# Streamed modulation summed on TensorE in four column blocks, and second buffers for the operands of a recurrent head

## The chip, the cores and the metric

The kernel runs on one core of one Trainium2 chip. The metric is the device time of one execution in microseconds (us); lower is better. "Before" was timed in three runs. Engines are named as the profile names them: PE is TensorE, DVE is VectorE, ACT is ScalarE, POOL is GpSimd, SP is SyncE, whose instruction queue issues nearly all DMAs of this kernel.

## What is computed

One step of a two-layer diffusion trunk over 512 sample tokens and 128 prompt tokens, 2048 features, all in float32. Each layer first turns a conditioning vector into a shift, a scale and a gate for every feature, once for the sample and once for the prompt:

```python
def modulate_and_norm(x, cond, w_mod, b_mod, g):
    m = (jax.nn.silu(cond) @ w_mod + b_mod)[:, None, :]
    shift, scale, gate = jnp.split(m, 3, axis=-1)
    return rmsnorm(x, g) * (1 + scale) + shift, gate
```

`w_mod` is [2048, 6144] in each layer, 50 MB, and it multiplies two vectors only. The first layer then has eight heads of latent attention and eight heads of a gated recurrence run in both directions (chunked scan: queries, values, two forget gates, a state per head), the second has sixteen heads of attention in a window; each ends in an output projection, a gate and a residual sum.

## The kernel before

Activations lie with features on the partitions and the 640 tokens along the row. Wide products run as `coltile`: 128 output columns at a time, in two *units* of eight 128-row weight tiles (512 KB). A unit's weights come by one DMA into a buffer of the pool `rawp` (four buffers, L149), are split into a high and a low part by one ACT copy (L75) and one DVE subtraction (L76), and are used by 48 matmuls of 320 columns in three passes (L113 to L115). The results gather in PSUM banks named `acc`.

The stages follow one another: the start (modulation of layer one for the features needed at once, `mod_tensor`, L267, and the first columns); the eight recurrent heads (`hgrn_head`); the latent attention; the output of layer one; layer two.

The change lies in the stage of the recurrent heads. A head needs five `coltile` products, ten units: two gates (evicted by ACT, L490, into the tile `e`), the query (evicted by DVE, L477, into `q`), the value (`v`, after a transpose) and the output gate. Between them stands its recurrence: some 60 elementwise operations of DVE and ACT, and small matmuls (L554, L556, L580, L611, L625 to L628) that each wait for DVE. Four levels of a doubling scheme follow one another: the small products of a level (L580), a masked copy (L552), then a multiplication of queries (L589) and keys (L590) by decays. `e` is overwritten by the keys and lives until the last transposes of the head; `e`, `q` and `v` have one buffer each, so the next head's gates can't be evicted before.

Beside the heads runs the *stream*: the modulation sums that are not needed at once, 4 blocks of 512 features of layer one and all 12 of layer two. `mod_sums` (L280) keeps them off PE. Each of its 128 pieces loads 512 KB into `mraw` (two buffers); for each of the two row tiles in it DVE multiplies by the sample's conditioning and adds (L295), ACT multiplies by the prompt's (L296) and POOL adds (L297). After eight pieces four matmuls against ones sum over the partitions (L302), one for each quarter of the accumulators, into four 32-column blocks of PE side by side; an ACT copy (L305) and two DMAs (L307) put the 512 sums in DRAM. `pump` (L320), called once a unit, advances the stream by eight pieces in five units.

The order of work within each engine is fixed when the program is built, by a scheduler that goes by program order and its own estimates of time; every engine, and the SP queue, then runs its list in order, waiting on semaphores. Weight splits are placed ahead of their place in the program (`ahead`). PSUM has eight banks; in this stage three are `acc`, three are for short-lived results (`w`) and two for the heads' outputs (`o`).

Of the kernel before, what the change touches and what calls it, by code (L numbers as in the profile page):

```python
# [14 lines left out]
P = 128  # L15
D = 2048
KT = 16
# [11 lines left out]
class Trunk:  # L29
# [20 lines left out]
    def rsqrt(self, out, v, tmp, add):  # L50
        """out = (v + add) ** -0.5; v may be in PSUM, tmp is scratch of the same shape."""
# [15 lines left out]
    def sigmoid(self, out, x):  # L67
        """out = 1 / (1 + exp(-x)), x bounded below."""
        nc = self.nc
        nc.scalar.activation(out, x, AF.Exp, scale=-1.0)  # L70
        nc.scalar.activation(out, out, AF.Ln, bias=self.bias_of(1.0, out.shape[0]))
        nc.scalar.activation(out, out, AF.Exp, scale=-1.0)
# [5 lines left out]
    def token_sums(self, pool, parts):  # L78
        """Sums over the features for (columns of ones [128, 32], squares [128, 640]) parts -> [128, 5], by token."""
# [15 lines left out]
    def unit(self, src, pool=None, **kw):  # L95
        """src: AP [128, k, n] in DRAM -> split tile [128, 2, k, n]."""
# [9 lines left out]
    def ahead(self):  # L106
        """What is emitted inside is scheduled before its place in the program."""
        return self.tc.high_priority(offset=400)

    def three(self, out, w, a, start, stop):  # L110
        """out (+)= w.T @ a with w, a = (hi, lo) pairs."""
# [5 lines left out]
    def coltile(self, w, c0, act, us=(0, 1), extra=0):  # L117
        """(w[:, c0:c0+128]).T @ act -> two PSUM tiles, the first with the extra leading columns of act."""
# [18 lines left out]
    def banked(self, **banks):  # L137
        """PSUM banks of a phase by use: w short-lived, o sums of heads, m modulation, acc wide products."""
# [6 lines left out]
    def setup(self):  # L145
# [22 lines left out]
        for l in ("ab", "c"):  # L168
            self.mod[l] = self.t(c, [P, 48, 2], tag=f"mod_{l}")
            # gains (1 + scale) * norm  # L170
            self.mod[l + "a"] = self.t(c, [P, 16, 2], tag=f"moda_{l}")

    def conditioning(self, tp):
        """silu of the two conditionings, as stationary columns 0 and 1."""
# [28 lines left out]
    def gains(self, tp):  # L203
# [24 lines left out]
        # lower bounds of the forget gates: softmax over the layer axis, cumulated, minus its first row  # L228
# [16 lines left out]
    def mod_done(self, l, f0, n, ps):  # L245
        """Feature tiles f0 .. f0+n from their sums in ps [128, n, 2]."""
# [10 lines left out]
    def mod_tensor(self, l, js):  # L257
        """Features 256*j .. on the tensor engine, four blocks of rows side by side; yields after each piece."""
# [21 lines left out]
    def mod_sums(self, l, js, pool):  # L280
        """Features 512*j .. summed over blocks of rows off the tensor engine; yields after each piece."""
        nc = self.nc
        wm = self.io[f"mod_w_{l}"][0].rearrange("(k p) c -> p k c", p=P)
        for j in js:
            acc = self.t(pool, [P, 2, 512], tag="macc")
            for kq in range(8):
                raw = self.t(pool, [P, 2, 512], tag="mraw", bufs=2)
                nc.sync.dma_start(raw, wm[:, 2 * kq:2 * kq + 2, 512 * j:512 * j + 512])
                for i in range(2):
                    s0, s1 = (self.sc[:, 2 * kq + i, c:c + 1] for c in range(2))  # L290
                    if kq + i == 0:
                        nc.vector.tensor_scalar(acc[:, 0], raw[:, i], scalar1=s0, scalar2=None, op0=ALU.mult)
                        nc.scalar.activation(acc[:, 1], raw[:, i], AF.Copy, scale=s1)
                    else:
                        nc.vector.scalar_tensor_tensor(acc[:, 0], raw[:, i], s0, acc[:, 0], op0=ALU.mult, op1=ALU.add)  # L295
                        nc.scalar.activation(raw[:, i], raw[:, i], AF.Copy, scale=s1)  # L296
                        nc.gpsimd.tensor_tensor(acc[:, 1], acc[:, 1], raw[:, i], op=ALU.add)  # L297
                if kq < 7:
                    yield
            ps = self.w()[:, :256]  # L300
            for g in range(4):
                nc.tensor.matmul(ps[32 * g:32 * g + 32, :], lhsT=self.ones[1.0][:, 0:32],  # L302
                                 rhs=acc[:, g // 2, 256 * (g % 2):256 * (g % 2) + 256], start=True, stop=True)
            row = self.t(pool, [P, 256], tag="mrow")
            nc.scalar.activation(row, ps, AF.Copy)  # L305
            for c in range(2):
                nc.sync.dma_start(self.mrow[c, 2 * j:2 * j + 2], row[64 * c:64 * c + 64:32])  # L307
            if j == 11:
                f0 = 4 * js[0]
                n = 48 - f0  # L310
                rows = self.t(pool, [2 * n, P], tag="mrows")
                for c in range(2):
                    nc.sync.dma_start(rows[n * c:n * c + n], self.mrow[c, 2 * js[0]:24].rearrange("a (i p) -> (a i) p", p=P))
# [6 lines left out]
    def pump(self):  # L320
        """One product unit passes: the share of the streamed modulation that goes with it."""
        if self.stream is not None:
            self.units += 1
            for _ in range(2 if self.units % 5 in (0, 2, 4) else 1):
                next(self.stream, None)

# [36 lines left out]
    def start(self):  # L363
# [6 lines left out]
        def columns(k0, k1, c):  # L370
            """Rows 128*k0 .. 128*k1 of w_in, one tile of the latent and gate columns."""
# [32 lines left out]
        def modulate(k):  # L404
            """h tile k (hi, lo)."""
# [26 lines left out]
    def latent_norm(self, xs, j0, gain):  # L432
        """Latent rows j0 .. normalised over the features, to DRAM."""
# [25 lines left out]
    def hgrn_setup(self, pool):  # L459
        nc, io = self.nc, self.io  # L460
        self.masks = self.t(pool, [P, 6, P], U8, tag="masks")
        stage = self.t(pool, [P, 6, P], tag="e")
# [8 lines left out]
    def evict_silu(self, pool, pts, tag):  # L471
        """(bounded x) * sigmoid(x) of a column tile."""
        nc = self.nc
        x = self.t(pool, [P, T], tag=tag)
# [849 lines left out]
```

## Time and profile before

| | us |
|---|---|
| runs timed | 2556.28, 2563.78, 2561.87 |
| median | 2561.87 |
| profiled execution, first to last instruction (its span; no other time of it is recorded) | 2554.8 |
| of it, the stage of the recurrent heads with the stream: first piece loaded to last sums read back | 849 (231 to 1080) |

The table's last row is a stretch of the profiled execution. Busy times, idle times and durations below all come from that one execution. A group row reads: line, engine, operation, tiles written and read, count, then busy time, mean duration, idle time just before and what ended it. A PE instruction's end is modelled and overlaps the next one's start, so the cost of a matmul in a row of them is read from the distance between starts. A float32 matmul appears as two records, one in the high-and-low product (L113 to L115) as one.

### The profile page before, as it was taken

The page shows a single profiled execution, that of the slowest core. Times are in us where ns is not written, and L with a number is a line of the kernel's source. Part 1 is how long each engine was busy: PE and PEld are TensorE (multiplying, and loading weights), DVE is VectorE, ACT ScalarE, POOL GpSimd, SP SyncE. Part 2 cuts the span into 40 slices and gives each one's busy share as a digit, 9 for nine tenths or more (in the row PEclk, how much of TensorE's full clock was granted, in tenths as well). Part 3 has the DMA queues.
Part 4 walks back from the last instruction along what each step waited for, and adds up shares of the span by engine and source line. Part 5 has one row for each costly group of instructions (what it writes and reads, how often), then busy time and mean ns, then how long its engine had stood idle before and what let it go on. Part 6 is the DMA issues. An engine that isn't in the chain of part 4 may idle for free.

```text
span 2554.8 us, 42083 instructions
## 1 busy us (share of the span) xinstructions
PE 2443.2 (96%) x16745; PEld 2319.2 (91%) x16745; DVE 1644.2 (64%) x3002; ACT 1088.2 (43%) x1979; POOL 465.2 (18%) x313
## 2 busy tenths in 40 slices
PE   7999898998989888999999999999999999999999
PEld 5789888888888888898898999999999999999999
DVE  4656889889888898857555566555555555564222
ACT  4224544554545445445444343344344343354211
POOL 1001545554545555300000012000000000000000
PEclk8999999999999999999999999999999999999999
DMA  9974444444444444454233355322222222225431
GB/s 309 303 246 153 139 124 144 136 143 128 137 133 148 138 128 136 121 147 141 72 99 100 110 189 157 108 72 72 84 77 74 82 73 70 80 55 165 120 116 58
DMA packets 409124, 324.94 MB, mean 127 GB/s; under 512 B 36218, under 2 KB 347936, under 8 KB 408416
## 3 DMA queue, kind: packets, MB, share of 16 engines
q1 hardware_dynamic: 408352, 322.17, 41.8%
q8 instruction: 131, 2.15, 0.3%
q14 instruction: 65, 0.53, 0.1%
q0 software_dynamic: 576, 0.09, 0.1%
HBM read 277.58 MB, written 36.76 MB: 123 GB/s over the span
## 4 chain that ended last, share of the span: by engine, by line
PE 57%; DVE 4%; DMA 1%; issue 1%; ACT 0%; POOL 0%; SPq 0%; DVEq 0%; POOLq 0%; ACTq 0%
PE acc L114 14%; PE acc L115 14%; PE acc L113 14%; PE w L48 2%; PE w L113 2%; PE o L1150 2%; PE w L115 2%; PE w L114 2%; PE o L897 1%; DVE macc L295 1%; PE w L874 1%; DVE split L76 1%; DMA mraw<-in_mod_w_c_dram 1%; PE w L84 0%; PE w L873 0%
## 5 line engine op out<-in xcount | busy, mean ns | idle before, releaser
L113 PE MATMUL acc<-act,split 128*128 128x320 f32 (+1 forms) x3552 | 1131.1, 319 | 29.1 <-DVE q L477 27.2
L115 PE MATMUL acc<-act,split 128*128 128x320 f32 (+1 forms) x3552 | 1122.9, 316 | 0.0
L114 PE MATMUL acc<-act,split 128*128 128x320 f32 (+1 forms) x3552 | 1122.6, 316 | 0.1
L113 PEld LDWEIGHTS acc<-act,split 128*128 128x128 f32 x3552 | 680.9, 192 | 63.6 <-DVE q L477 29.3
L114 PEld LDWEIGHTS acc<-act,split 128*128 128x128 f32 x3552 | 680.2, 192 | 6.9 <-issue 2.7
L115 PEld LDWEIGHTS acc<-act,split 128*128 128x128 f32 x3552 | 680.4, 192 | 5.8 <-issue 3.3
L297 POOL TENSOR_TENSOR macc<-macc,mraw 128x512 f32<-128x512 f32 x240 | 411.7, 1716 | 390.4 <-ACT mraw L296 250.4
L75 ACT ACTIVATE split<-raw 128x1024 fp32r<-128x1024 f32 (+4 forms) x297 | 284.3, 957 | 433.5 <-PE acc L115 412.9
L76 DVE TENSOR_TENSOR split<-raw,split 128x1024 fp32r<-128x1024 f32 (+4 forms) x297 | 348.7, 1174 | 182.1 <-ACT split L75 174.9
L295 DVE SCALAR_TENSOR_TENSOR macc<-mraw,sc,macc 128x512 f32<-128x512 f32 x240 | 246.7, 1028 | 65.9 <-DMA mraw<-in_mod_w_c_dram 44.0
L296 ACT ACTIVATE mraw<-mraw,sc 128x512 f32<-128x512 f32 x240 | 172.7, 722 | 240.5 <-DVE macc L295 194.7
L580 PE MATMUL w<-lf,km 128*128 128x128 f32 x320 | 46.7, 298 | 40.9 <-DVE lf L589 40.6
L1133 ACT ACTIVATE sc<-sc,mxc,rqc 128x512 f32<-128x512 f32 (+2 forms) x80 | 56.1, 701 | 67.2 <-DVE mxc L1132 67.1
L580 PEld LDWEIGHTS w<-lf,km 128*128 128x128 f32 x320 | 41.7, 205 | 46.6 <-ACT mraw L296 23.7
L114 PE MATMUL acc<-mc,split 128*128 128x320 f32 x256 | 80.2, 314 | 0.2 <-DVE mc L76 0.2
L113 PE MATMUL acc<-mc,split 128*128 128x320 f32 x256 | 79.1, 314 | 0.0
L115 PE MATMUL acc<-mc,split 128*128 128x320 f32 x256 | 79.0, 309 | 0.0
L113 PE MATMUL acc<-mixa,split 128*128 128x320 f32 x256 | 78.8, 308 | 0.0
L114 PE MATMUL acc<-mixa,split 128*128 128x320 f32 x256 | 78.8, 308 | 0.0
L115 PE MATMUL acc<-mixa,split 128*128 128x320 f32 x256 | 78.7, 308 | 0.0
L388 DVE TENSOR_TENSOR lat<-lat,acc 128x320 f32<-128x320 f32 (+1 forms) x72 | 34.9, 485 | 58.4 <-PE acc L115 58.1
L648 DVE TENSOR_TENSOR swc<-swc,tabC 128x512 f32<-128x512 f32 x20 | 13.9, 693 | 85.3 <-DMA swc<-qc 69.1
(395 smaller groups left out, 3478.6 us busy)
## 6 DMA issues: line engine op xcount, KB each, us to landing
mraw<-in_mod_w_c_dram SPq DMA_DIRECT2D x96, 512.0 KB
raw<-in_w_in_ab_dram SPq DMA_DIRECT2D x92, 512.0 KB
raw<-in_w_in_c_dram SPq DMA_DIRECT2D x80, 512.0 KB
raw<-in_mod_w_ab_dram SPq DMA_DIRECT2D x64, 512.0 KB
mraw<-in_mod_w_ab_dram SPq DMA_DIRECT2D x32, 512.0 KB
raw<-in_w_out_ab_dram SPq DMA_DIRECT2D x32, 512.0 KB
raw<-in_w_out_c_dram SPq DMA_DIRECT2D x32, 512.0 KB
raw<-in_w_in_ab_dram SPq DMA_DIRECT2D x24, 256.0 KB
```

Source lines behind the costliest of these rows:

```text
L48: self.nc.tensor.transpose(out, in_, self.ident[:k, :k])
L75: self.nc.scalar.activation(hi, full, AF.Copy)
L76: self.nc.vector.tensor_tensor(lo, full, hi.bitcast(F32), op=ALU.subtract)
L113: mm(out, lhsT=w[0], rhs=a[0], start=start, stop=False)
L114: mm(out, lhsT=w[0], rhs=a[1], start=False, stop=False)
L115: self.last = mm(out, lhsT=w[1], rhs=a[0], start=False, stop=stop).ins
L295: nc.vector.scalar_tensor_tensor(acc[:, 0], raw[:, i], s0, acc[:, 0], op0=ALU.mult, op1=ALU.add)
L296: nc.scalar.activation(raw[:, i], raw[:, i], AF.Copy, scale=s1)
L297: nc.gpsimd.tensor_tensor(acc[:, 1], acc[:, 1], raw[:, i], op=ALU.add)
L580: select(PS, 2 + li, lambda o, c: nc.tensor.matmul(o.rearrange("p (n d m) -> p n d m", d=2, m=m), lhsT=km[:, P * c:P * c + P], rhs=pairs(Q ...
L1133: nc.scalar.activation(s, s, AF.Exp, bias=mx[:, 2:3], scale=rq[:, b:b + 1], accum_out=mx[:, 0:1])
L1150: nc.tensor.matmul(od, lhsT=v[:, k0 // P + c], rhs=pT[:, c], start=c == 0, stop=c == nb - 1)
```

## The change

`mod_sums` is replaced by `mod_blocks`. A block is now 1024 features, and there are 2 + 6 of them. For each of the 16 row tiles of a block one DMA loads 128 x 1024 weights (512 KB, as before) into a `rawp` buffer, shared with the product weights, and four matmuls multiply it by the two conditioning columns (padded to 32), each quarter of 256 features into another 32-column block of PE; the sum over row tiles is made in one PSUM bank. DVE, ACT and POOL have no part in it. Two row tiles make a piece, 64 pieces in all; `pump` now advances by one piece in four units of five. The bank for it, `m`, is taken from `acc`, which goes from three to two. `e`, `v` and `q` get a second buffer.

```diff
-    def mod_sums(self, l, js, pool):
+    def mod_blocks(self, l, bs, pool):
         nc = self.nc
         wm = self.io[f"mod_w_{l}"][0].rearrange("(k p) c -> p k c", p=P)
-        for j in js:
-            acc = self.t(pool, [P, 2, 512], tag="macc")
-            for kq in range(8):
-                raw = self.t(pool, [P, 2, 512], tag="mraw", bufs=2)
-                nc.sync.dma_start(raw, wm[:, 2 * kq:2 * kq + 2, 512 * j:512 * j + 512])
-                for i in range(2):
...
-                        nc.vector.scalar_tensor_tensor(acc[:, 0], raw[:, i], s0, acc[:, 0], op0=ALU.mult, op1=ALU.add)
-                        nc.scalar.activation(raw[:, i], raw[:, i], AF.Copy, scale=s1)
-                        nc.gpsimd.tensor_tensor(acc[:, 1], acc[:, 1], raw[:, i], op=ALU.add)
-                if kq < 7:
+        for b in bs:
+            ps = self.w("m")[:, :256]
+            for k in range(KT):
+                raw = self.t(self.rawp, [P, 1024], tag="raw")
+                nc.sync.dma_start(raw, wm[:, k, 1024 * b:1024 * b + 1024])
+                for g in range(4):
+                    nc.tensor.matmul(ps[32 * g:32 * g + 32, :], lhsT=self.sc[:, k, :], rhs=raw[:, 256 * g:256 * g + 256],
+                                     start=k == 0, stop=k == KT - 1)
+                if k % 2 and k < KT - 1:
                     yield
-            ps = self.w()[:, :256]
-            for g in range(4):
-                nc.tensor.matmul(ps[32 * g:32 * g + 32, :], lhsT=self.ones[1.0][:, 0:32],
-                                 rhs=acc[:, g // 2, 256 * (g % 2):256 * (g % 2) + 256], start=True, stop=True)
             row = self.t(pool, [P, 256], tag="mrow")
             nc.scalar.activation(row, ps, AF.Copy)
...
     def pump(self):
         if self.stream is not None:
             self.units += 1
-            for _ in range(2 if self.units % 5 in (0, 2, 4) else 1):
+            if self.units % 5:
                 next(self.stream, None)
...
-        stage = self.t(pool, [P, 6, P], tag="e")
+        stage = self.t(pool, [P, 6, P], tag="e", bufs=2)
...
-        x = self.t(pool, [P, T], tag=tag)
+        x = self.t(pool, [P, T], tag=tag, bufs=2 if tag == "q" else 1)
...
-        e = t([P, 2, T], "e")
+        e = t([P, 2, T], "e", bufs=2)
...
-        v = t([P, 5, P], "v")
+        v = t([P, 5, P], "v", bufs=2)
...
-            with self.banked(acc=3, w=3, o=2):
+            with self.banked(acc=2, w=3, o=2, m=1):
...
-                    self.stream = chain(self.mod_sums("ab", range(8, 12), bp), self.mod_sums("c", range(12), bp))
+                    self.stream = chain(self.mod_blocks("ab", range(4, 6), bp), self.mod_blocks("c", range(6), bp))
```

Where PE passes from the value product of the second head to its gate product, before has the last matmuls of one unit and the first of the next; `split_3835` and `split_4073` are the two units' weights.

```order
L114 MATMUL acc_3763<-act_2026,split_3835 128x320
L115 MATMUL acc_3763<-act_2026,split_3835 128x320
L113 MATMUL acc_4069<-act_477,split_4073 128x320
L114 MATMUL acc_4069<-act_477,split_4073 128x320
L115 MATMUL acc_4069<-act_477,split_4073 128x320
```

At the same place after, `m_3306` is the block's PSUM bank and `raw_4011` and `raw_4017` are its last two row tiles; x4 stands for the four quarters.

```order
L114 MATMUL acc_3698<-act_2026,split_3766 128x320
L115 MATMUL acc_3698<-act_2026,split_3766 128x320
L48 MATMUL w_3832<-ident_70,vr_3696 128x128 x2
L290 MATMUL m_3306<-raw_4011,sc_129 32x256 x4
L290 MATMUL m_3306<-raw_4017,sc_129 32x256 x4
L113 MATMUL acc_4004<-act_477,split_4008 128x320
```

One piece, eight matmuls, now stands between two units. The program has 128 groups of four such matmuls, in 73 uninterrupted runs: 56 whole pieces, seven that the scheduler parted after the fifth matmul, and one in three parts.

The SP queue, in the same head, loads the weights of units (L100) and the pieces of the stream (L288) before into buffers of their own:

```order
L288 DMA mraw_3546<-in_mod_w_ab_dram 128x2x512
L288 DMA mraw_3554<-in_mod_w_ab_dram 128x2x512
L100 DMA raw_4325<-in_w_in_ab_dram 128x8x128
L288 DMA mraw_3619<-in_mod_w_ab_dram 128x2x512
L100 DMA raw_4398<-in_w_in_ab_dram 128x8x128
L288 DMA mraw_3627<-in_mod_w_ab_dram 128x2x512
```

and after into the four buffers of `rawp` in turn (L1185 stores a finished head, L1194 before):

```order
L288 DMA raw_3628<-in_mod_w_ab_dram 128x1024
L288 DMA raw_3634<-in_mod_w_ab_dram 128x1024
L100 DMA raw_3699<-in_w_in_ab_dram 128x8x128
L288 DMA raw_3704<-in_mod_w_ab_dram 128x1024
L1185 DMA mix_28_108<-mix_3270 128x640
L288 DMA raw_3710<-in_mod_w_ab_dram 128x1024
L100 DMA raw_3764<-in_w_in_ab_dram 128x8x128
```

Each load now waits for the use of the one four loads earlier: a split on DVE where that was a weight, matmuls on PE where it was a piece.

On DVE, one level of the second head's recurrence before, with the stream's sums (L295) among its steps; `PS` gathers the masked products, `lf` holds the queries, `e` the keys:

```order
L552 COPY_PREDICATED PS_3929<-masks_2424,w_3956 128x384
L552 COPY_PREDICATED PS_3929<-masks_2424,w_3961 128x256
L589 TENSOR_TENSOR lf_3907<-lf_3907,TT_3918 128x2x40x8
L295 SCALAR_TENSOR_TENSOR macc_3697<-mraw_4076,sc_129,macc_3697 128x512
L479 TENSOR_TENSOR gate_4224<-gate_4224,sil_4225 128x640
L590 TENSOR_TENSOR e_3343<-e_3343,TT_644_3982 128x2x10x32
```

and after (lines L543, L580, L581 and L468 are before's L552, L589, L590 and L477):

```order
L543 COPY_PREDICATED PS_3864<-masks_2424,w_3891 128x384
L543 COPY_PREDICATED PS_3864<-masks_2424,w_3896 128x256
L580 TENSOR_TENSOR lf_3842<-lf_3842,TT_3853 128x2x40x8
L581 TENSOR_TENSOR e_3298<-e_3298,TT_639_3917 128x2x10x32
L468 TENSOR_SCALAR gate_4134<-acc_4005 128x320
```

The sums are gone from DVE's list; the steps of the recurrence stand in the same order.

More of the change, by code (lines that the diff above doesn't have):

```diff
@@ L278, in mod_tensor @@
             yield
-    def mod_sums(self, l, js, pool):
+    def mod_blocks(self, l, bs, pool):
         nc = self.nc
         wm = self.io[f"mod_w_{l}"][0].rearrange("(k p) c -> p k c", p=P)
-        for j in js:
-            acc = self.t(pool, [P, 2, 512], tag="macc")
-            for kq in range(8):
-                raw = self.t(pool, [P, 2, 512], tag="mraw", bufs=2)
-                nc.sync.dma_start(raw, wm[:, 2 * kq:2 * kq + 2, 512 * j:512 * j + 512])
-                for i in range(2):
[L290 to L297, printed above, removed]
-                if kq < 7:
+        for b in bs:
[7 more added lines that the diff above has]
+                if k % 2 and k < KT - 1:
                     yield
-            ps = self.w()[:, :256]
-            for g in range(4):
-                nc.tensor.matmul(ps[32 * g:32 * g + 32, :], lhsT=self.ones[1.0][:, 0:32],
-                                 rhs=acc[:, g // 2, 256 * (g % 2):256 * (g % 2) + 256], start=True, stop=True)
             row = self.t(pool, [P, 256], tag="mrow")
@@ L306, in mod_sums @@
             for c in range(2):
-                nc.sync.dma_start(self.mrow[c, 2 * j:2 * j + 2], row[64 * c:64 * c + 64:32])
-            if j == 11:
-                f0 = 4 * js[0]
+                nc.sync.dma_start(self.mrow[c, 4 * b:4 * b + 4], row[c:P:32])
+            if b == 5:
+                f0 = 8 * bs[0]
                 n = 48 - f0
@@ L312, in mod_sums @@
                 for c in range(2):
-                    nc.sync.dma_start(rows[n * c:n * c + n], self.mrow[c, 2 * js[0]:24].rearrange("a (i p) -> (a i) p", p=P))
+                    nc.sync.dma_start(rows[n * c:n * c + n],
+                                      self.mrow[c, 4 * bs[0]:24].rearrange("a (i p) -> (a i) p", p=P))
                 ps = self.w()
```

## The prediction

> **What bounds the kernel now.** I read the page's first two parts, then the busy times by stretch, the waits of PE, and the groups that the change removes. From the page, busy time by engine, and per slice of 64 us in tenths:
>
> ```profile
> span 2554.8 us, 42083 instructions
> PE 2443.2 (96%) x16745; PEld 2319.2 (91%) x16745; DVE 1644.2 (64%) x3002; ACT 1088.2 (43%) x1979; POOL 465.2 (18%) x313
> ...
> PE   7999898998989888999999999999999999999999
> ...
> DVE  4656889889888898857555566555555555564222
> ...
> POOL 1001545554545555300000012000000000000000
> PEclk8999999999999999999999999999999999999999
> ```
>
> PE is the engine that is nearly always busy, except in slices 4 to 17, the stage of the recurrent heads. There DVE is at eight and nine tenths and POOL, idle elsewhere, at five. So what the change is worth is decided in that stage. Its ends are the first load of a piece and the last read of the sums; the stretch table puts it beside three stretches of the latent attention:
>
> ```profile
> L288 SPq DMA_DIRECT2D mraw<-in_mod_w_ab_dram x32: 367/368/1120, 231.4 to 434.6; - x32
> L313 SPq DMA_DIRECT2D mrows<-mrow x4: 330/341/359, 450.4 to 1080.5; - x4
> ```
> ```profile
> core 0: us, PE busy (x) PEld busy (x) DVE busy (x) ACT busy (x) POOL busy (x), PEclk, DMA share, GB/s
> 231.00:1080.00 849.00, 760.08 (x5040) 729.62 (x5039) 745.37 (x885) 420.42 (x608) 421.08 (x257) 0.95 0.46 139
> 1200.00:1300.00 100.00, 98.28 (x652) 88.74 (x652) 57.08 (x153) 44.29 (x96) 0.00 (x0) 0.98 0.31 89
> 1300.00:1400.00 100.00, 99.96 (x679) 89.40 (x679) 56.33 (x146) 44.10 (x93) 0.00 (x0) 1.00 0.34 100
> 1400.00:1500.00 100.00, 100.00 (x691) 93.06 (x690) 58.29 (x156) 44.45 (x99) 0.96 (x2) 1.00 0.43 138
> ```
>
> In 849 us PE is idle for 88.9, and its granted clock is 0.95 on the mean against 1.00 where it never waits. Whom it waits for, in the stage alone:
>
> ```profile
> PE w L580 <- DVE lf L589: 40.6, 23, 2.8
> PE acc L113 <- DVE q L477: 27.2, 8, 5.6
> PE w L302 <- DVE macc L295: 14.5, 6, 2.9
> ```
>
> All three name DVE. The stream's own work, and what it does to DVE's other work, shows in groups and in the spread (least, median, longest ns) of single lines:
>
> ```profile
> L297 POOL TENSOR_TENSOR macc<-macc,mraw 128x512 f32<-128x512 f32 x240 | 411.7, 1716 | 390.4 <-ACT mraw L296 250.4
> L295 DVE SCALAR_TENSOR_TENSOR macc<-mraw,sc,macc 128x512 f32<-128x512 f32 x240 | 246.7, 1028 | 65.9 <-DMA mraw<-in_mod_w_c_dram 44.0
> ```
> ```profile
> L295 DVE SCALAR_TENSOR_TENSOR macc<-mraw,sc,macc x240: 728/752/1877, 238.5 to 1069.2; 128x512 f32<-128x512 f32 x120
> ```
> ```profile
> L590 DVE TENSOR_TENSOR e<-e,TT x32: 807/815/1915, 313.0 to 1056.7; 128x640 f32<-128x640 f32 x32
> ```
> ```profile
> L590 DVE TENSOR_TENSOR e<-e,TT 128x640 f32<-128x640 f32 x32 | 41.2, 1288 | 0.0
> ...
> L407 DVE TENSOR_TENSOR xn<-xT,R 128x640 f32<-128x640 f32 x16 | 12.8, 814 | 0.0
> ```
>
> A DVE operation takes either its median or some 1.1 us more; L590, no part of the stream, has a mean of 1.29 against a median of 0.82. L407, of the same form in the start stage where POOL adds nothing, has a mean of 0.81. So I take the longer mode for DVE waiting on POOL. The Trainium skill ("SBUF — State Buffer", the section on its two separate sides) says that DVE and GpSimd share one port pair that is locked for a whole instruction, so that the other blocks. The two modes in these rows agree with it.
>
> **Part by part.** First the work of PE at full clock, without any wait. A clock of 0.95 between full and half means a tenth of 849 at half speed, 85 us; PE is busy in 0.90 of the stage, so 76 busy us did 38 us' work. That leaves 760 - 38 = 722 us.
>
> The sum over partitions goes:
>
> ```profile
> L302 PE MATMUL w<-macc,ones 128*32 128x256 f32 x128 | 17.0, 422 | 16.4 <-DVE macc L295 14.5 <-DVE TT L593 1.8 <-POOL macc L297 0.2
> ```
> ```profile
> 656.86 0.64 PE L302 MATMUL w<-macc,ones 128*32 128x256 f32 x8
> ```
>
> 17 us less: 705. Added are 512 matmuls of 256 columns in four blocks. The start stage has the same form, two groups of four in a run between wide matmuls, and one group alone (start, duration):
>
> ```profile
> 77.48 0.31 PE L115 MATMUL acc<-act,split 128*128 128x320 f32 x1
> ...
> 78.36 0.31 PE L115 MATMUL acc<-act,split 128*128 128x320 f32 x1
> 78.60 1.07 PE L267 MATMUL m<-raw,sc 128*32 128x256 f32 x16
> 79.60 0.42 PE L113 MATMUL acc<-act,split 128*128 128x320 f32 x1
> 79.86 0.31 PE L114 MATMUL acc<-act,split 128*128 128x320 f32 x1
> ...
> 81.90 0.64 PE L267 MATMUL m<-raw,sc 128*32 128x256 f32 x8
> 82.47 0.41 PE L113 MATMUL acc<-act,split 128*128 128x320 f32 x1
> ```
>
> Six wide matmuls take 78.36 - 77.48 = 0.88, one 0.147. From 78.36 to 79.86 are 1.50; two steps of 0.147 would be there anyway, so a piece costs 1.21, of which 79.60 - 78.60 = 1.00 is matmul and 0.21 goes at the two changes of form. A group alone takes 0.57, so the second adds 0.43. 64 pieces cost 77 us; nine more runs, from the eight pieces that are parted, cost 0.57 + 0.21 each, 7 us. In all 84, and PE's work becomes 705 + 84 = 789. That all four quarters now use the same stationary columns is no new case: L302 did so too, and its eight records took 0.64 like L267's.
>
> The Trainium skill ("TensorEngine Tiling (Array Packing)", Key Properties) has a rule against this change: a change of tiling mode drains TensorE. The 0.21 in the rows is that price, and it agrees that there is one. The same skill ("TensorE: Matmul & The Clock Gate", on the measured speedup of packing) counts a group as one matmul's duration and 4 ns for each further tile; with the 0.43 above that is 0.44, 56 us in all by that rule, an estimate 28 below mine. The sum keeps the rows' 84.
>
> Now what hides and what waits. DVE loses 246.7 us of sums, 745 - 247 = 498 are left, and less where lengthened operations shrink to their medians: L590 alone would give 32 x (1.29 - 0.82) = 15. ACT and POOL only lose work. So the wait L302 <- L295 goes whole; L113 <- q goes because L477 no longer stands behind late sums; L580 <- L589 shrinks. DVE at 498 of some 800, 62%, is near the 56 to 58% of the three attention stretches, which also run with two `acc` banks. I take their PE as the measure: idle 1.72 + 0.04 + 0 of 300 us, 0.6%, and a clock mean of 0.993, 0.7% lost; 1.3% of 789 is 10 us, and the worst stretch (1.72 idle, 2 lost) would make 29. The recurrence is a longer chain than anything there, so I take 16.
>
> The third `acc` bank costs nothing by these stretches; its cover is 24 wide matmuls, 24 x 0.147 = 3.5 us, between the end of a half product and the reuse of its bank. If an eviction came later, PE would wait for the rest. The second buffers act on one thing that the rows show, gates of the next head that can't be evicted:
>
> ```profile
> ACT e L490 <- PE w L48: 11.9, 7, 6.5
> ACT e L490 <- DVE masks L464: 5.4, 1, 5.4
> ```
>
> These are ACT's waits and partly PE's idle time above; I count no more for them. DMA bytes stay; the SP queue has 16 small stores (L307) fewer. Its large loads take, in the chain of the longest pieces (start, us):
>
> ```profile
> 951.80 3.69 DMA mraw<-in_mod_w_c_dram
> ...
> 979.36 4.74 DMA mraw<-in_mod_w_c_dram
> ...
> 1022.88 5.18 DMA mraw<-in_mod_w_c_dram
> ```
>
> The second load of each piece is freed by PE, at the piece before, and is due one unit and a group later: 48 x 0.147 + 1.2 = 8.3 us. With 5.2 it is hidden with 3.1 to spare; a weight's load has two units.
>
> The sum: the stage becomes 789 + 16 = 805 in place of 849, 44 us less; nothing after it changes but its start. The span of 2554.8 becomes 2511. The median of the runs is 7.1 above the profiled span, and the same is kept: 2561.9 - 44 = 2518.
>
> **Rivals.** (1) *The waits are the recurrence itself, not DVE's load.* Then L580 keeps its 40.6 us and with it about half the lost clock, 19: the stage is 789 + 41 + 19 = 849, and the time stays at 2562. Half of it gives 819, 30 below, 2532; two thirds 829, 20 below. For it: the two levels' steps (L589, then L580) alternate with no slack on paper. Against: L590's modes, and that of the 32 levels (four in each of eight heads) only 23 wait even now, 2.8 at most. I hold a remainder more likely than the whole.
>
> (2) *Slower: the stream starves PE.* Loads of weights and pieces now share four buffers and stand in one queue; a store that waits, such as L1185's, holds both. The queue's waits in the stage:
>
> ```profile
> SPq L288 <- POOL macc L297: 334.6, 118, 8.4
> SPq L100 <- DVE split L76: 251.3, 68, 7.5
> ```
>
> It already waits most of the time, at worst 7.5 to 8.4 us. The point is 8.3: a load of 5.2 that starts more than 3.1 late stops PE, and at 1 us per piece the 60 us between 849 and 789 are used up. At 2 us per piece it is 789 + 128 = 917, 68 more: 2630. Against: the queue waits now because two `mraw` buffers are freed by POOL last, and that goes.
>
> (3) *The four blocks don't run side by side in this form.* Then a row tile costs 4 x 0.43: 128 x 1.72 = 220 in place of 55, the stage 970, 2683. L302 speaks clearly against it.
>
> **How the numbers follow.** A measurement of this kernel can tell about 0.3%, 7.7 us, from no change. The forecast with its unknowns, 27 to 70 us gained, has 0.62; a larger remainder of rival 1, 8 to 27 us gained, 0.21; within 7.7 us, rival 1 whole, 0.06; slower, rivals 2 and 3, 0.11. So faster 0.83. The low end takes no waits (849 - 789 = 60) and no price for the changes of form (64 x 0.21 = 13): 73, and 2490 with rounding. The high end, 2555, is where faster ends; above lie 0.17, below some 0.02.
>
> **What would show it.** In the changed kernel the stage of the heads should be near 805 us with PE over 97% busy and a clock of 0.98 or more; POOL near nothing; DVE's L590 (then L581) close to 0.82 on the mean; a run of 16 records of the new matmuls 1.0 to 1.1 us; PE's wait for lf under 15 us. I am wrong on the chain if that wait stays near 40, on the queue if PE waits for a DMA into `raw` for more than some us, on the price if a run of 16 takes longer than 1.2.

## The result, and the profile after

| | before | after |
|---|---|---|
| median of four runs each (us) | 2562.8 | 2482.4 |
| lowest to highest | 2556.3 to 2565.3 | 2480.8 to 2485.5 |
| profiled execution: its span, its own time | 2554.8, 2556.3 | 2479.9, 2481.6 |

The ratio of the times is 0.9686, with a 95% interval from 0.9669 to 0.9703. The change brings 80 us by the medians and 75 us by the two spans; the profiled execution of before was the lowest of its four runs. The forecast was 2518 with a range of 2490 to 2555, so the sign was right and the gain was put at little more than half of its size.

The page of the changed kernel, in the parts that were shown of before:

```profile
span 2479.9 us, 42698 instructions
PE 2456.6 (99%) x17641; PEld 2305.0 (93%) x17641; DVE 1316.1 (53%) x2746; ACT 917.0 (37%) x1715; POOL 54.3 (2%) x73
...
PE   7999999999999999999999999999999999999999
...
DVE  5545555555555456565555565555555545554221
...
POOL 1000000000000000000000022000000000000000
PEclk8999999999999999999999999999999999999999
```

The dip of PE in slices 4 to 17 is gone, and so is POOL there. The same 849 us that held the stage before, now of the changed kernel, with the columns of that table, and after it the whole list of PE's waits between 225 and 1080 us:

```profile
231.00:1080.00 849.00, 848.69 (x6416) 790.45 (x6415) 456.84 (x691) 285.27 (x398) 10.27 (x17) 1.00 0.49 150
```
```profile
PE w L48 <- ACT vr L485: 0.2, 1, 0.2
```

88.9 us of idle time have become 0.3, and the clock 1.00 in place of 0.95. The stage itself is shorter than those 849 us now: the last matmul of the heads (L628 before, L619 after) starts at 1003.8 and not at 1082.5 us, 78.7 earlier, so in the forecast's terms the stage takes 770 and not 805; the end of the stretch already lies in the latent attention. Where before had L580 waiting for `lf` 23 times, `acc` for `q` eight times and the sums six times, the list names none of them. The DVE line whose two lengths the prediction started from, and a piece of the new matmuls between wide ones (start, duration):

```profile
L581 DVE TENSOR_TENSOR e<-e,TT x32: 815/818/826, 305.2 to 980.1; 128x640 f32<-128x640 f32 x32
```
```profile
605.03 0.30 PE L115 MATMUL acc<-act,split 128*128 128x320 f32 x1
605.26 1.07 PE L290 MATMUL m<-raw,sc 128*32 128x256 f32 x16
606.26 0.41 PE L113 MATMUL acc<-act,split 128*128 128x320 f32 x1
606.51 0.31 PE L114 MATMUL acc<-act,split 128*128 128x320 f32 x1
```

The longest of 32 is 826 ns where it was 1915. The piece takes 606.51 - 605.03 = 1.48, less two steps of 0.147: 1.19, where the forecast had 1.21.

### The profile page after: what moved, and what is told of

It reads as the page before. It is cut to its first block, busy times and chain, and to the rows that moved or that the text cites. A ratio compares the mean times of both kernels' runs of the same rounds, so it can differ in the third digit from the quotient of the medians.

```text
span 2479.9 us, 42698 instructions
## 1 busy us (share of the span) xinstructions
PE 2456.6 (99%) x17641; PEld 2305.0 (93%) x17641; DVE 1316.1 (53%) x2746; ACT 917.0 (37%) x1715; POOL 54.3 (2%) x73
## 4 chain that ended last, share of the span: by engine, by line
PE 96%; DMA 3%; DVE 0%; ACT 0%; issue 0%; SPq 0%; DVEq 0%; ACTq 0%
PE acc L113 25%; PE acc L115 24%; PE acc L114 24%; PE w L48 3%; PE m L290 3%; PE w L113 2%; PE o L1141 2%; PE w L115 2%; PE w L114 2%; DMA raw<-in_mod_w_ab_dram 2%; PE o L888 1%; PE m L267 1%; PE w L571 1%; PE w L865 1%; PE w L602 1%; DMA raw<-in_w_in_ab_dram 1%
## 5 line engine op out<-in xcount | busy, mean ns | idle before, releaser
L113 PEld LDWEIGHTS acc<-act,split 128*128 128x128 f32 x3552 | 670.7, 189 | 57.5 <-issue 28.0
L115 PEld LDWEIGHTS acc<-act,split 128*128 128x128 f32 x3552 | 668.9, 188 | 6.8 <-issue 3.3
L114 PEld LDWEIGHTS acc<-act,split 128*128 128x128 f32 x3552 | 669.5, 188 | 4.6 <-issue 1.6
L76 DVE TENSOR_TENSOR split<-raw,split 128x1024 fp32r<-128x1024 f32 (+4 forms) x297 | 326.8, 1100 | 329.9 <-ACT split L75 327.4
L115 PE MATMUL acc<-mixa,split 128*128 128x320 f32 x256 | 78.7, 308 | 0.0
L543 DVE COPY_PREDICATED PS<-masks,w 128x384 f32<-128x384 uint8 x80 | 37.8, 514 | 68.2 <-PE w L571 48.1
L290 PE MATMUL m<-raw,sc 128*32 128x256 f32 x1024 | 73.6, 386 | 0.0
L1119 DVE CUSTOM_DVE_ANT_0 sc<-w,band 128x512 f32<-128x512 f32 (+2 forms) x80 | 43.5, 554 | 35.4 <-PE w L115 35.3
L1141 PE MATMUL o<-pTc,vc 128*128 128x128 f32 x448 | 57.9, 275 | 0.0
L917 DVE SCALAR_TENSOR_TENSOR y<-acc,mod_c,y 128x320 f32<-128x320 f32 (+2 forms) x48 | 19.4, 437 | 72.4 <-PE acc L115 72.4
```

The source lines that it names most:

```text
L76: self.nc.vector.tensor_tensor(lo, full, hi.bitcast(F32), op=ALU.subtract)
L113: mm(out, lhsT=w[0], rhs=a[0], start=start, stop=False)
L114: mm(out, lhsT=w[0], rhs=a[1], start=False, stop=False)
L115: self.last = mm(out, lhsT=w[1], rhs=a[0], start=False, stop=stop).ins
L290: nc.tensor.matmul(ps[32 * g:32 * g + 32, :], lhsT=self.sc[:, k, :], rhs=raw[:, 256 * g:256 * g + 256], start=k == 0, stop=k == KT - 1)
L543: nc.vector.copy_predicated(dst[:, c0:c1], self.masks[:, mi].unsqueeze(1).to_broadcast([P, c1 - c0, P]), p[:, :P * (c1 - c0)].rearrange("p ...
```

## The experiments

The theory under test was this. *POOL's additions lengthen DVE's operations (the two modes of L590), the in-order chain of the stream does the rest, and PE waits for both.* The first rival: the waits belong to the recurrence. The second: it is DVE's load, whoever lengthens it. A third, which came up on the way: it isn't contention between the two engines, but POOL's place as the last link that frees the stream's buffers. Where no number of runs is given, a kernel ran once. Runs of one kernel lay 5 to 12 us apart, so a difference of a few us between single runs is not read as an effect.

**1. The second buffers.** The changed kernel with one buffer again for `e`, `q` and `v`:

```diff
-        e = t([P, 2, T], "e", bufs=2)
+        e = t([P, 2, T], "e")
-        v = t([P, 5, P], "v", bufs=2)
+        v = t([P, 5, P], "v")
```

(and so for `q` and the staging tile.)

> The changed kernel with one buffer each for e, q and v, as before; all else as changed. Changed kernel: span 2479.9 us, before 2554.8. Theory (the gain is DVE and POOL freed from the stream, the second buffers add little): span 2480 to 2492, PE's waits in the stage of the heads under 10 us. Rival (the second buffers made the gain, since the next head's gates couldn't be evicted): PE waits for e or q come back, span 2515 or more.

Measured: 2483.8 (four runs), ratio to before 0.9696 (0.9674 to 0.9718), span 2483.4. The intervals of the two kernels overlap for the most part. That part of the change brings nothing that can be measured, as counted; the whole gain is the stream's.

**2. POOL alone taken away.** The kernel before without L297, so that the prompt's sums are left out; ACT's product L296 stays.

```diff
                         nc.scalar.activation(raw[:, i], raw[:, i], AF.Copy, scale=s1)
-                        nc.gpsimd.tensor_tensor(acc[:, 1], acc[:, 1], raw[:, i], op=ALU.add)
```

> The kernel before without POOL's additions (L297), so the prompt's sums are left out; DVE and ACT keep their part of the stream, and PE has no modulation but the sum over partitions. Theory A (DVE is late because its operations wait for POOL): L590 falls from 1.29 to about 0.82 us and L295 from 1.03 to 0.75, PE's 82 us of waits for DVE mostly go, span 2480 to 2505. Theory B (DVE is late by the number of its operations): the operations may shorten, but PE still waits over 50 us, span 2530 or more.

Measured: 2420.7, span 2418.9, which is 136 us less than before and far below the number expected. The stretch from 231 us to near the stage's end, and the line of the two modes (L589 here):

```profile
231.00:1020.00 789.00, 782.87 (x5554) 766.50 (x5553) 611.67 (x952) 455.65 (x666) 10.27 (x17) 1.00 0.56 163
```
```profile
L589 DVE TENSOR_TENSOR e<-e,TT x32: 809/823/844, 306.8 to 924.7; 128x640 f32<-128x640 f32 x32
```

DVE still does its 240 sums and is busy for 612 of 789 us, 78%, yet PE is idle for 6.1 us only and the clock is 1.00. So nearly all of the loss hung on POOL's 240 additions, and DVE's own load, which stays, costs little without them. The rival of DVE's load falls for this load, and so does the rival of the recurrence.

**3. DVE's sums alone taken away.** The kernel before without L295, so that the sample's sums are left out; ACT and POOL go on.

```diff
-                        nc.vector.scalar_tensor_tensor(acc[:, 0], raw[:, i], s0, acc[:, 0], op0=ALU.mult, op1=ALU.add)
```

> The kernel before without DVE's 240 multiply-adds of the stream (L295), so the sample's sums are left out; ACT and POOL keep theirs. Theory A (waiting for POOL): L590 stays near 1.3 us and PE still waits 30 to 60 us, span 2510 to 2540. Theory B (number of operations): DVE loses 247 us, PE's waits go, span 2490 or less.

Measured: 2510.2, span 2508.5: 46 less than before, where taking POOL's part away gave 136. The span is just under theory A's 2510 to 2540, but the row that A named did not stay near 1.3 us:

```profile
L589 DVE TENSOR_TENSOR e<-e,TT 128x640 f32<-128x640 f32 x32 | 30.4, 949 | 31.8 <-ACT km L578 31.8
```

PE's waits in the stage:

```profile
PE w L579 <- DVE lf L588: 19.8, 7, 4.2
PE w L301 <- POOL macc L296: 17.0, 8, 3.1
PE w L48 <- ACT vr L493: 12.1, 7, 3.3
PE w L579 <- ACT km L578: 10.2, 6, 4.0
```

They are spread over DVE, POOL and ACT now, and ACT itself stands before its products:

```profile
ACT mraw L295 <- DMA mraw<-in_mod_w_c_dram: 159.6, 69, 5.6
```

That row suggested the third rival: POOL frees the `mraw` buffers late, the load is late, ACT stands before it in order, and the recurrence's steps on ACT queue behind. Experiment 4 was to decide between the two.

**4. POOL busy, but outside of the stream.** The kernel of experiment 1, where nothing of the stream is on POOL, with 256 additions of two tiles that nobody else uses:

```diff
                 next(self.stream, None)
+                for _ in range(4):
+                    self.nc.gpsimd.tensor_tensor(self.idle_a, self.idle_a, self.idle_b, op=ALU.add)
```

> The changed kernel with single buffers, and 256 additions of 128x512 on GpSimd that wait for nothing and that nobody waits for; they can run one behind the other from the stage's start, so for some 440 us GpSimd is as busy as it can be. If what made TensorE wait was that GpSimd's operations lengthen VectorE's (contention by itself): VectorE's operations in that stretch take some 1.1 us more each, TensorE's waits for lf and q come back with 30 us or more, half-clock stretches too: span 2515 or more. If it was GpSimd's place in the stream, as the link that frees the buffers: VectorE's operations are longer all the same, but TensorE's waits stay under 10 us and the span is within 10 of 2483.

Measured: 2548.0, span 2546.3 against 2483.4: 63 us for additions that no instruction waits for. The expectation that I held, POOL's place in the chain as the whole cause, fell. They ran one behind the other, and so the run holds its own comparison, the first 400 us against the next 400, in the columns of the stretch table; and DVE's groups, first with POOL busy (230 to 630), then with POOL silent (730 to 1080):

```profile
230.00:630.00 400.00, 353.87 (x2597) 323.04 (x2596) 296.10 (x264) 110.25 (x151) 377.75 (x234) 0.95 0.43 133
630.00:1030.00 400.00, 394.48 (x3025) 364.25 (x3024) 229.17 (x325) 126.84 (x177) 58.63 (x40) 1.00 0.50 153
```
```profile
L76 DVE TENSOR_TENSOR split<-raw,split 128x1024 fp32r<-128x1024 f32 x37 | 70.6, 1911 | 46.0 <-ACT split L75 46.0
L583 DVE TENSOR_TENSOR e<-e,TT 128x640 f32<-128x640 f32 x12 | 20.1, 1674 | 1.2 <-ACT km L572 1.2
...
L545 DVE COPY_PREDICATED PS<-masks,w 128x384 f32<-128x384 uint8 (+1 forms) x30 | 14.2, 513 | 11.5 <-PE w L547 7.3 <-PE w L573 4.0
```
```profile
L76 DVE TENSOR_TENSOR split<-raw,split 128x1024 fp32r<-128x1024 f32 x38 | 46.5, 1223 | 67.1 <-ACT split L75 66.6
L545 DVE COPY_PREDICATED PS<-masks,w 128x384 f32<-128x384 uint8 (+1 forms) x40 | 19.0, 515 | 32.8 <-PE w L573 22.7 <-PE w L547 9.7
L583 DVE TENSOR_TENSOR e<-e,TT 128x640 f32<-128x640 f32 x16 | 13.1, 820 | 1.6 <-ACT km L572 1.6
```

With POOL busy the split of a weight takes 1911 ns and not 1223, the recurrence's step 1674 and not 820; the masked copy is the same in both, 513 and 515. PE is idle for 46 of the first 400 us and for 5.5 of the next, in whose first 57 POOL's additions end, and only in the first does the clock fall. Its largest waits in the stage are again those for `q` and `lf`:

```profile
PE acc L113 <- DVE q L470: 29.5, 8, 7.5
PE w L573 <- DVE lf L582: 14.3, 8, 2.3
```

That is the theory's own contention, shown without the chain. The Trainium skill ("SBUF — State Buffer", the section on its two separate sides) has DVE and GpSimd share a port pair under an exclusive lock; that some operations double while another is untouched agrees with a lock that only some operations need, though no run here shows which port it is.

**5. The same additions, spread.** Each four of them wait for a tiny ACT copy of their piece, so that they don't run all at once:

```diff
                 next(self.stream, None)
+                self.nc.scalar.activation(self.idle_b[:, 0:1], self.sc[:, 0, 0:1], AF.Copy)
                 for _ in range(4):
```

> The changed kernel with single buffers and 256 free additions of 128x512 on GpSimd, as in the run with span 2546, but each four of them wait for a tiny ScalarE copy of their piece, so that they are spread over the stage as the additions of the kernel before were; nobody waits for them but the next copy's write. Contention by itself, with as many additions: 50 to 65 us as before, span 2530 to 2550, and VectorE's lines of the recurrence are lengthened over the whole stage (L583 mean 1.1 to 1.3). If spread additions find VectorE between its operations, less than 25 us are left: span under 2510; what the kernel before lost beyond that was then the chain through GpSimd and VectorE's load of sums.

Measured: 2557.2, span 2555.5, 72 us above 2483.4; as large as expected of contention, a little more than the range. The spread came out small: most of the stretch from 231 to 730 us still had POOL busy.

```profile
L319 POOL TENSOR_TENSOR idle_a<-idle_a,idle_b 128x512 f32<-128x512 f32 x256 | 416.4, 1627 | 56.2 <-ACT idle_b L317 41.7
```

So this run is a second measurement of the same price rather than a test of spacing.

**6. The same elements in shorter additions.** Each addition of experiment 4 is cut into four of 128x128.

```diff
-                for _ in range(4):
-                    self.nc.gpsimd.tensor_tensor(self.idle_a, self.idle_a, self.idle_b, op=ALU.add)
+                for i in range(16):
+                    part = slice(128 * (i % 4), 128 * (i % 4) + 128)
+                    self.nc.gpsimd.tensor_tensor(self.idle_a[:, part], self.idle_a[:, part], self.idle_b[:, part], op=ALU.add)
```

> As the run with 256 free additions on GpSimd (span 2546, L583 1674 ns in the stretch with them against 820 without), but each addition of 128x512 is cut into four of 128x128: the same elements in shorter instructions. If a VectorE operation has to let a whole GpSimd instruction pass (the lock lasts an instruction), the wait per VectorE operation becomes about a third to a quarter, 0.2 to 0.4 us in place of 0.85, L583 near 1.0 to 1.2, and the span 2490 to 2520. If it is only shared bandwidth, the same elements cost the same: L583 stays near 1.6 in that stretch and the span at 2535 to 2560.

Measured: 2598.2, span 2596.4: both expectations fell, it is 50 us worse than with long additions. POOL's group, a DVE line of the recurrence (least, median, longest), PE's first wait, and one moment on DVE (start, duration):

```profile
L319 POOL TENSOR_TENSOR idle_a<-idle_a,idle_b 128x128 f32<-128x128 f32 x1024 | 568.3, 596 | 0.0
```
```profile
L556 DVE TENSOR_TENSOR lf<-lf,E x8: 1482/1510/39857, 325.5 to 1080.4; 128x1280 f32<-128x1280 f32 x8
```
```profile
PE w L574 <- ACT km L573: 54.6, 3, 35.4
```
```profile
637.22 39.86 DVE L556 TENSOR_TENSOR lf<-lf,E 128x1280 f32<-128x1280 f32 x1
677.00 1.74 DVE L557 TENSOR_TENSOR e<-e,E 128x1280 f32<-128x1280 f32 x1
```

An operation of 1.5 us took 39.86, while at 568.3 / 1024 = 0.555 us apiece some 72 additions of POOL went by; and PE waited 35 us for what followed. The median is not longer, 1510. It is no single case: ten more DVE operations of this stage, all with two tensor inputs, took 5 to 15 us. So a DVE operation does not wait for one POOL instruction and then have its turn. It can be passed over many times, and POOL's next instruction always being ready makes that worse. What decides who gets the turn is not shown.

**7. No stream at all.** The kernel before without loads and sums of the stream; it leaves out the modulation of the later layers.

```diff
-                    self.stream = chain(self.mod_sums("ab", range(8, 12), bp), self.mod_sums("c", range(12), bp))
+                    self.stream = iter(())
```

> The kernel before with no stream at all: neither its loads nor its sums; it leaves out the modulation of the later layers, whose tables are zero. Theory: the recurrence by itself makes TensorE wait for under 10 us; the stage is TensorE's own work at full clock, 785 to 800 us: span 2400 to 2415. Rival (half of the waits belong to the recurrence): some 40 us of waits and half clock remain, span 2437 or more.

Measured: 2400.4, span 2398.6.

```profile
231.00:1000.00 769.00, 769.00 (x5433) 764.39 (x5432) 457.51 (x693) 287.14 (x398) 10.28 (x17) 1.00 0.29 80
```

Without the stream the recurrence makes PE wait for nothing at all. The first rival is out.

**8. The price of the new matmuls.** The changed kernel with the matmuls of the first row tile of each block only; it leaves out 15 of 16 parts of the sums, and every load stays.

```diff
-                for g in range(4):
+                for g in range(4 if k == 0 else 0):
```

> The changed kernel with the modulation matmuls of the first of each 16 row tiles alone; all loads stay, so 15 of 16 parts of the modulation's sums are left out. If PE's work sets the stage and 128 groups cost the 84 us worked out before: 15/16 of it goes, 79 us, span 2401. If something else sets it (loads, the recurrence), the span falls by less than 50, to 2430 or more.

Measured: 2416.8, span 2415.0, between the two expectations and nearer the first: 120 of the 128 groups of four cost 2479.9 - 2415.0 = 65 us, not 79. The eight groups that stay are 15 short runs, since seven of them are parted, and a run of part of a group takes as long as a group alone, 0.70 to 0.76 us by the starts around it: some 11 us. The stream's loads, which all stay, cost next to nothing: experiment 7 has neither loads nor sums and is 16 below, and without those 11 us some 5 are left for the 67 MB of loads, no more than runs of one kernel differ by.

**9. The banks.** The kernel before with two banks for `acc` and four for `w`:

```diff
-            with self.banked(acc=3, w=3, o=2):
+            with self.banked(acc=2, w=4, o=2):
```

> The kernel before with two banks for acc and four for the short tiles, as the changed kernel has them; the stream stays as it was. Theory: the third bank is worth little, 0 to 5 us; the span stays at 2550 to 2562. Rival: with the evictions as late as they are in this stage, the third bank hides them, and without it TensorE's wait for q grows from 27 to 45 us or more: span 2570 to 2590.

Measured: 2580.3 (four runs), ratio 1.0069 (1.0050 to 1.0089): slower by 13 to 23 us. PE's first waits in the stage:

```profile
PE acc L113 <- DVE q L477: 61.2, 8, 8.1
PE w L580 <- DVE lf L589: 36.5, 19, 3.5
```

The wait for `q` has grown from 27.2 to 61.2 us, as the rival said. As long as DVE is late the third bank hides part of it; in the changed kernel, with two, the same wait isn't there. Here a bank has a price only beside the lateness that it covers.

**10 and 11. A version that may beat both.** If POOL was the harm, DVE may keep part of the stream. In experiment 10 DVE multiplies and adds for both conditionings, in half of the stream, and the other half stays in blocks on PE (single buffers):

```diff
+                        nc.vector.scalar_tensor_tensor(acc[:, 0], raw[:, i], s0, acc[:, 0], op0=ALU.mult, op1=ALU.add)
+                        nc.vector.scalar_tensor_tensor(acc[:, 1], raw[:, i], s1, acc[:, 1], op0=ALU.mult, op1=ALU.add)
...
-            if self.units % 5:
-                next(self.stream, None)
+            for s in ((1,), (0,), (1,), (0, 0), (0,))[self.units % 5]:
+                next(self.stream[s], None)
...
-                    self.stream = chain(self.mod_blocks("ab", range(4, 6), bp), self.mod_blocks("c", range(6), bp))
+                    self.stream = (chain(self.mod_sums("ab", range(8, 12), bp), self.mod_sums("c", range(4), bp)),
+                                   self.mod_blocks("c", range(2, 6), bp))
```

> The changed kernel with single buffers for e, q and v, where half of the stream (eight of the sixteen features' columns groups of 512) is summed by VectorE alone, both conditionings, with nothing on ScalarE or GpSimd, and the other half stays on TensorE in four blocks. Theory (GpSimd as the slowest link of the stream made the waits, not VectorE's load): VectorE is at about 85% of the stage and TensorE still waits for under 10 us; half the matmuls of the stream go, 36 to 39 us less, while some 10 us of sums over partitions come back: stage about 840, span 2445 to 2460, under 2470 in any case. Rival (VectorE's load itself made the waits): at 85% VectorE the waits for lf, q and the sums come back with 40 us or more and the half clock with them: span 2480 to 2530, no better than the changed kernel.

Measured: 2471.5 (five runs), ratio 0.9647 (0.9626 to 0.9667), span 2468.0. The stage's stretch and PE's largest wait:

```profile
231.00:1080.00 849.00, 838.04 (x6061) 792.48 (x6060) 622.88 (x978) 299.30 (x420) 10.29 (x17) 1.00 0.52 155
```
```profile
PE acc L113 <- DVE q L506: 8.5, 7, 2.3
```

It is the fastest version that computes everything, 11 us below the changed kernel by the medians, with DVE at 73% of that stretch. Its span is still 8 above the range expected: PE idles for 11, and half of the stream with its sums over partitions costs 2468.0 - 2398.6 - 11 = 58, not some 46 (half of 81, and 5 of L300's busy time). The trace has its groups in 59 uninterrupted runs, where the changed kernel has 73 for nearly twice as many groups. Experiment 11 puts three quarters on DVE:

```diff
-            for s in ((1,), (0,), (1,), (0, 0), (0,))[self.units % 5]:
+            for s in ((1,), (0,), (0, 0), (0,), (0, 0))[self.units % 5]:
```

> As the version with half of the stream on VectorE (2471.5, TensorE waits 9 us in the stage), with three quarters of it there and one quarter on TensorE. TensorE's own work falls by another 18 to 20 us; VectorE's busy share in the stage goes from 73 to about 86%. Theory (VectorE's load costs little while GpSimd is silent): waits grow by under 10 us, span 2452 to 2465. Rival (past three quarters VectorE's load makes waits): waits for q, lf and the sums grow by 20 us or more and half the clock with them: span 2470 to 2500, no gain over the half.

Measured: 2488.3 (five runs), ratio 0.9709 (0.9696 to 0.9723), span 2485.3. That is 17 us above the half by the medians and 6 above the changed kernel, whose interval of the ratio (0.9669 to 0.9703) it overlaps: no gain over it.

```profile
231.00:1080.00 849.00, 813.11 (x5735) 776.22 (x5735) 685.79 (x1072) 286.60 (x401) 10.28 (x17) 0.99 0.51 150
```
```profile
PE w L609 <- DVE lf L618: 11.2, 4, 4.0
PE acc L113 <- DVE q L506: 10.8, 8, 3.4
PE w L609 <- ACT km L608: 7.8, 6, 1.8
```

With DVE at 81% PE is idle for 36 us, and the rival was right here: DVE's load makes waits too, without any help of POOL. What the matmuls give back is eaten by them. One caution: experiment 2 had DVE at 78% and 6 us, so where it turns depends on how the sums lie as well as on the share.

## Why the prediction was right in sign and wrong in size

The sum went from the span 2554.8 to 2511. The same four terms, measured with spans:

| term | forecast | measured | from |
|---|---|---|---|
| the waits and the clock they cost | -127 (88.9 + 38) | -142 | experiment 2: 2554.8 - 2418.9 + 6.1 still idle |
| the sum over partitions, L302 | -17 | -14 | 2418.9 - 6.1 - 2398.6 |
| the new matmuls | +84 | +81 | after against experiment 7: 2479.9 - 2398.6 |
| waits and clock that stay | +16 | 0 | the idle 0.3 us of the stage after |
| span | -44 | -75 | |

Experiments 2 and 7 ran once, so a row stands to within some 5 us; the profiled execution of before was the lowest of its runs, so the first row is rather too small than too large. Experiment 7 has no loads either, so the second and third rows each hold what the stream's loads cost, some 5 us at most by experiment 8.

- **That the waits were not the recurrence's own** was right, and so was the row it was read from: L590's two modes are POOL's work. They are gone without its additions (experiment 2) and come with additions that do nothing else (experiment 4). What weighed was misjudged, though. The prediction counted the 247 us of sums that DVE loses and took the shrinking of lengthened operations as an extra of which it named 15. In experiment 2 DVE keeps all its sums and PE still idles for 6.1 us only.
- **"I take 16"** is the first step that failed. It was taken from attention stretches, and raised because "the recurrence is a longer chain than anything there". Without POOL's additions and DVE's sums PE waits for nothing in it: 0.3 us. Here the length of the chain said nothing, because other work of PE stands between its steps. In the changed kernel 48 wide matmuls of a unit lie between two pumps, and DVE is now done before PE comes for it. The prediction had the rows for that: 32 levels, of which only 23 waited even before, 2.8 us at most.
- **The cost of the waits** is the second, 15 too little. A mean clock of 0.95 in two digits stands for a share at half speed between 0.09 and 0.11 of 849 us, which is 34 to 42 us of lost work; that explains 4 of the 15 at most. The rest then lies in time that the profile counts as busy, whose ends are modelled on PE; no run splits it further. A pair of runs with and without the cause showed it, a page of the profile by itself could not.
- **The price of the matmuls** was right, and on the way it was got: 81 by spans, loads included, and 1.19 in place of 1.21 for a piece. The Trainium skill's count of a packed group ("TensorE: Matmul & The Clock Gate", on the measured speedup of packing) made an estimate of 56 of it, with the 0.43 of a row put in. It leaves out what a run of groups costs at its ends: 1.19 - 2 x 0.43 = 0.33 for each of 73 runs, 24 us, and some 3 for eight groups that are parted and so cost twice. That there is a price at each change of form agrees with the drain that the Trainium skill names ("TensorEngine Tiling (Array Packing)", Key Properties); whether all of the 0.33 is that drain, no run here shows.
- **"The same is kept"** added 7.1 us between span and median. The profiled execution of before was its lowest run; after, the median is 2.5 above the profiled span. That is 4.6 us more, and with the 31 of the spans it makes the 35.6 between 2518 and 2482.4.
- **The banks** cost nothing where evictions are on time, as said, and the condition named with it counts: in experiment 9, where evictions are late, the missing bank costs 13 to 23 us. The change would have looked worse had it been made in two steps.
- **Rivals.** The larger remainder of the recurrence (0.21) and the whole of it (0.06) got chances that experiment 7 leaves nothing of. The starved PE didn't come: no load of `raw` is in PE's waits of the stage. Blocks that don't run side by side are out by the 1.07 us of a run of 16.
- **The range** ended at 2490 because its low end took the base work, 722 of PE at full clock, as known. It was the unknown that mattered most, as large as either of the two that were varied. No waits left would by themselves have given 2502, inside the range; what carried the time out of it was the cost of the waits, 15 too little, with the 4.6 of the median.

How the 142 us divide is answered only in part. POOL's additions by themselves, with nobody waiting for them, cost 63 and 72 (experiments 4 and 5). In the stream, without DVE's sums, they cost 2508.5 - 2398.6 - 14 = 96, though DVE's operations are lengthened less there (L589 has a mean of 949 ns over the stage, where the free additions of experiment 4 gave L583 1247). So ACT's products and the late loads may add some 25 to 33 or more; that part is argued, not shown. DVE's sums beside POOL add the remaining 46, while without POOL they cost 6. Together they cost more than the sum of each alone, and no single share belongs to either.

## What to carry to other kernels

When two lengths of one instruction stand in a profile, look for the engine whose busy stretches they go with, and try the kernel without that engine's work before costing anything else: here 240 additions on an engine at 18% cost 136 of 2555 us. Moving off PE a sum that PE does in 81 us is a gain only if the engines that take it don't slow those that feed PE; here taking part of it on DVE alone was better than both. And when a wait is caused by another engine, don't keep a remainder of it as prudence: either a row shows what remains, or it is zero and belongs into the range.

## What the runs showed of the hardware that was not expected

- Short POOL instructions in an unbroken row hurt DVE more than long ones with the same elements: 113 us above the run without them (2596.4 against 2483.4) where long ones cost 63. One DVE operation took 39.86 us where the median of its line is 1.51.
- DVE's masked copy (`COPY_PREDICATED`, 128x384 and 128x256) is not lengthened by POOL at all, 513 and 515 ns, while two-input operations go from 820 to 1674 and from 1223 to 1911.
- POOL's addition of 128x128 takes 0.555 us apiece on the mean and of 128x512 1.667, both beside DVE's work, so four short ones cost a third more than one long one.
